# Low parts of the gate, branch, output and first MLP weights by an adding transfer from GpSimd

## Chip, cores, metric

One NeuronCore of a Trainium2 chip runs the whole program. The metric is device microseconds of one execution, the median of a few executions. Each execution computes one layer of a decoder for 512 tokens of width 1024 in float32.

## What is computed

Cut to the parts that the change touches; every product of activations and weights in it is a float32 matmul with inner dimension 512 or 1024.

```
h = rmsnorm(x, g_mix);  u = h @ w_in            # latents, pool, SSD, RG-LRU columns, and 4 x 1024 gate columns
y_a, y_b, y_c, y_d = attention, pooling, SSD, RG-LRU     # each 512 wide
gates = sigmoid(u[gate columns])
merged = sum over n of gates[n] * (y[n] @ w_branch[n])    # branch n: 512 x 1024
x = x + merged @ w_out
x = x + square(relu(rmsnorm(x, g_mlp) @ w_ff1)) @ w_ff2   # 1024 x 4096, 4096 x 1024
x = x + (p @ w_ple) * sigmoid(rmsnorm(x, g_ple) @ w_ple_gate)
out = rmsnorm(x, g_final)
```

## The kernel before

Every float32 matrix is split into a rounded part of type float32r, which TensorE takes at its fast rate, and the rest, also float32r: a = ah + al. A product is then three matmuls (helper `mm3`: high by high, high by low, low by high). In the trace they stand as lines L208, L209 and L210. Where the weight is the stationary operand, L208 and L209 read the weight's high tile `wh`, and only L210 reads its low tile `wl`.

The weights come in numbered units of 128 x 1024 (512 KB), in a fixed order (`UNITS`): latents, z and small projections, the gates of branch 0, the branch weights of 0 (`("br", 0, 0)` to `("br", 0, 3)`), then the LRU and pool projections mixed with the gates and branch weights of branch 2, then gates and branch weights of branches 3 and 1 in the pattern gate, branch, gate (one branch unit serves two output tiles), then 8 output units, then four chunks of the MLP. A chunk has 8 units of the first MLP matrix (`ff1`) and then a T phase: 14 units of the second matrix, which other code (`right_operand`, L192 and L193) splits from tiles `b` that SP loads. Units carry their number in the list below: 47 is the fourth gate of branch 2, 64 the second branch unit of branch 3, 70 its last, 87 the fourth output unit; 114, 136 and 158 are the first `ff1` units of chunks 1, 2 and 3, and 118 is the fifth of chunk 1.

`load_next` loads a unit: SP transfers it into `wr` (two buffers, L176), ScalarE rounds it into `wh` (three buffers, L177), VectorE subtracts, wl = wr - wh (three buffers, L178). `unit` calls it so that loading runs two units ahead of use. With three buffers of `wh` and `wl`, ScalarE can round a unit only once TensorE has left an older one. The framework decides the order on every engine beforehand from a modelled timeline, with the loads at high priority; each engine then runs its list strictly in order and waits on semaphores.

GpSimd (POOL) before has only elementwise work: the sum of the gated branches (L439), two products in the LRU and pooling (L764, L774, L805), and two differences of `b` tiles per quarter chunk for the T phase (L903, L904).

Of the kernel before, what the change touches and what calls it, by code (L numbers as in the profile page):

```python
# [10 lines left out]
F32 = mybir.dt.float32  # L11
F32R = mybir.dt.float32r
I32 = mybir.dt.int32
AF = mybir.ActivationFunctionType
ALU = mybir.AluOpType
# [37 lines left out]
UNITS = []  # L53
UIDX = {}
# [72 lines left out]
def trunk(tc, xT, pT, pos, par_d, cst_d, gfin, wblk_d, wpool_d, W, out, dbg=None):  # L127
    nc = tc.nc
    act, dve, pool, pe, sync = nc.scalar, nc.vector, nc.gpsimd, nc.tensor, nc.sync
    TAGS = {"G1": 16, "G2": 16, "G3": 16, "T1": 6, "T2": 8, "T3": 6, "Z": 4, "X": 8}  # L130
    BANKS = {"m": 3, "s": 2, "t": 2, "o": 1}
    with ExitStack() as ctx:
# [8 lines left out]
        def nm(s):  # L141
            cnt[0] += 1
            return f"{s}_{cnt[0]}"

        def A(tag, dt=F32, n="a"):
            return ap_.tile([P, S], dt, name=nm(n), tag=tag, bufs=TAGS[tag])
# [18 lines left out]
        def load_next():  # L165
            u = state[0]
            state[0] += 1
            n = UNITS[u][1]
            if UNITS[u][0][0] == "T":
                loaded[u] = right_operand(*UNITS[u][0][1:])  # L170
                return
            with tc.high_priority():
                raw = wp.tile([P, 1024], F32, name=nm("wr"), tag="wr", bufs=2)
                hi = wp.tile([P, 1024], F32R, name=nm("wh"), tag="wh", bufs=3)
                lo = wp.tile([P, 1024], F32R, name=nm("wl"), tag="wl", bufs=3)
                sync.dma_start(out=raw[:, :n], in_=W[u, :, :n])  # L176
                act.copy(out=hi[:, :n], in_=raw[:, :n])  # L177
                dve.tensor_tensor(out=lo[:, :n], in0=raw[:, :n], in1=hi[:, :n].bitcast(F32), op=ALU.subtract)  # L178
            loaded[u] = (hi, lo)


# [3 lines left out]
        def right_operand(ch, name, v):  # L185
            hi = wp.tile([P, 1024], F32R, name=nm("wh"), tag="wh", bufs=3)
            lo = wp.tile([P, 1024], F32R, name=nm("wl"), tag="wl", bufs=3)
            with tc.high_priority():
                for u in range(2):
                    kp, c = 2 * v + u, slice(u * S, (u + 1) * S)  # L190
                    src = ff2_raw[ch, {"t2": "b11", "t3": "b12", "t4": "b21"}.get(name, name), kp]
                    act.copy(out=hi[:, c], in_=src)  # L192
                    dve.tensor_tensor(out=lo[:, c], in0=src, in1=hi[:, c].bitcast(F32), op=ALU.subtract)  # L193
                    if name == "b11":
                        dve.tensor_tensor(out=src, in0=ff2_raw[ch, "b22", kp], in1=ff2_raw[ch, "t1", kp], op=ALU.subtract)
                    elif name == "b21":
                        dve.tensor_tensor(out=src, in0=src, in1=ff2_raw[ch, "b11", kp], op=ALU.subtract)
            return hi, lo

        def unit(*key):  # L200
            u = UIDX[key]
            while state[0] <= min(u + LOOK, NRING - 1):
                load_next()
            return loaded.pop(u)
# [16 lines left out]
        def pc(name, i=0, w=1):  # L221
            o, _ = PAR[name]
            return par[:, o + i:o + i + w]
# [93 lines left out]
        for k in range(KD):  # L317
            if k:
                sync.dma_start(out=xres[k], in_=xT[:, k, :])
            if k < 3:  # L320
                load_next()
            if k == 2:
                sync.dma_start(out=cst, in_=cst_d)
            xg.append(split_scaled(xres[k], pc("gmix", k), "G1", "xg"))
            q = A("T3", F32, "sq")
            act.activation(out=q, in_=xres[k], func=AF.Square)
            if acc is None:
                acc = q
            else:
                dve.tensor_tensor(out=acc, in0=acc, in1=q, op=ALU.add)  # L330
        for k in range(KD):
            if k == 5:
                with tc.high_priority():
                    vx = SM(NT, "vx")
                    dve.tensor_scalar(out=vx, in0=token_sums(acc), scalar1=1.0 / D, scalar2=EPS,
                                      op0=ALU.mult, op1=ALU.add)
                    rxb = bcast_tokens(rsqrt(vx, NT), "T1")
            w = loaded.pop(UIDX[("lat", k)])
            for i in range(5):
                c = slice(i * P, (i + 1) * P)  # L340
                mm3(lat_ps[i], w[0][:, c], w[1][:, c], xg[k][0], xg[k][1], k == 0, k == KD - 1)
            if k + 3 < KD:
                load_next()
# [7 lines left out]
        for k in range(KD):  # L351
            n = A("T3", F32, "hn")
# [118 lines left out]
        for t in range(NT):  # L471
# [3 lines left out]
                          in1=pc("dtb", 0, 8).unsqueeze(1).to_broadcast([P, NT, 8]), op=ALU.add)  # L475
# [75 lines left out]
        for hd in range(H):  # L551
# [11 lines left out]
            for kt in range(NT):  # L563
                pt = PS("t")
                n = S - kt * P
# [22 lines left out]
            else:  # L588
# [11 lines left out]
                                 in1=ah.unsqueeze(1).to_broadcast([P, NT, 8]), op0=ALU.mult, op1=ALU.mult)  # L600
# [18 lines left out]
        def bc8(v, n=8):  # L619
            return v.unsqueeze(2).to_broadcast([v.shape[0], n, 64])  # L620
# [4 lines left out]
        def csl(c):  # L625
            return slice(c * P, (c + 1) * P)
# [19 lines left out]
        for g in range(2):  # L646
            ps = PS("s")
            gs = slice(g * 64, g * 64 + 64)
            for c in range(NT):
                pe.matmul(ps[:, csl(c)], lhsT=xbc[4][gs, csl(c)], rhs=xbc[5][gs, csl(c)], start=True, stop=True)  # L650
            dve.tensor_tensor(out=heads(cbm[g], P), in0=heads(ps, P), in1=U.unsqueeze(1).to_broadcast([P, NT, P]),
                              op=ALU.mult)
        gate(0, 6, "G1")
        for c in range(NT):
            for g in range(2):
# [4 lines left out]
                for j in range(4):  # L660
# [4 lines left out]
                                   in1=cbm[g][:, csl(c)].unsqueeze(1).to_broadcast([P, 4, P]), op=ALU.mult)  # L665
# [4 lines left out]
        for c in range(NT - 1):  # L670
# [5 lines left out]
            for g in range(2):  # L676
# [4 lines left out]
                else:  # L681
                    dve.tensor_tensor(out=heads(Rn[gs, 0:256]), in0=heads(R[c][gs, 0:256]),
                                      in1=bc8(etot[gs, c * 8 + g * 4:c * 8 + g * 4 + 4], 4), op=ALU.mult)
# [3 lines left out]
        for c in range(NT):  # L687
# [7 lines left out]
            if c > 0:  # L695
                for g in range(2):
# [5 lines left out]
                                      in1=bc8(eacs[:, c * 8 + g * 4:c * 8 + g * 4 + 4], 4), op=ALU.mult)  # L702
# [93 lines left out]
        for i in range(4):  # L796
            w = unit("pool", i)
            ps = proj(w, hh, KD)
            u = A("T3", F32, "pu")
            act.copy(out=u, in_=ps)  # L800
            src = u
            n = 1
# [148 lines left out]
        for hf in range(2):  # L951
            ws = []
            for k in range(KD):
                raw = A("T1", F32, "pgw")
# [11 lines left out]
        for hf in range(2):  # L966

            for j in range(0, KD, 2):
                ps = PS("t")
                for u in range(2):  # L970
                    for t in range(2):
                        k = j + u
                        pe.transpose(out=ps[:, (2 * u + t) * P:(2 * u + t + 1) * P],
                                     in_=xt[2 * hf + t][k // 4][:, (k % 4) * P:(k % 4 + 1) * P], identity=ident)
# [28 lines left out]
        for hf in range(2):  # L1003
            ws = pgs[hf]
            for t in range(NT):
# [6 lines left out]
                for q in range(nf):  # L1012
# [3 lines left out]
                    for k in range(KD):  # L1016
# [9 lines left out]
                                                          in1=gf[:, hf, c], op=ALU.mult)  # L1026
# [146 lines left out]
```

## Time and profile before

| | |
|---|---|
| median of 3 runs | 981.22 us (980.24 to 982.66) |
| profiled execution | 982.21 us, its span 980.4 us: 1.8 us lie around the span |
| TensorE busy | 954.9 us, 97% of the span |
| VectorE, ScalarE, GpSimd busy | 661.4, 489.4 and 138.8 us |
| transfers | 96.95 MB, 29.5% of 16 DMA engines' time on SP's queue |

The share of the span says how much of the time an engine had work; the waits say what it waited for otherwise. Matmul ends are modelled, so TensorE's pace is better read from the starts of its rows.

### The profile page before, as it was taken

What the parts mean: (1) busy time and instruction counts of PE and PEld (TensorE: products, weight loads), DVE (VectorE), ACT (ScalarE), POOL (GpSimd) and SP (SyncE); (2) the same over time, 40 slices, a digit from 0 to 9 for tenths busy, and PEclk for the clock granted to TensorE, in tenths of its full rate; (3) what the DMA queues carried; (4) which work ended last, traced back from release to release, by engine and by line L of the source; (5) the groups of instructions that cost most, each with busy time, mean ns of one, the idle gap of its engine ahead of it and who ended that gap; (6) DMA issues with size and microseconds to landing.
All of it is one profiled execution on the core that took longest, in us unless ns stands there. A gap on an engine that the chain in (4) does not pass through costs nothing.

```text
span 980.4 us, 12002 instructions
## 1 busy us (share of the span) xinstructions
PE 954.9 (97%) x4389; PEld 782.4 (80%) x4389; DVE 661.4 (67%) x1156; ACT 489.4 (50%) x860; POOL 138.8 (14%) x107
## 2 busy tenths in 40 slices
PE   7999999999999999999999999999999999999996
PEld 5877788877777887788888888788887888887785
DVE  7768787557885753443433656996897789689636
ACT  6755777768276333222332435543543453456633
POOL 0000000005102423311122001350013005000021
PEclk9999999999999999999999999999999999999998
DMA  5423221214112332332324326134133304424002
GB/s 201 136 76 103 78 74 65 66 44 151 65 65 86 119 108 84 108 108 87 129 86 151 108 76 226 65 129 150 65 101 126 108 31 142 139 81 134 1 1 86
DMA packets 36473, 96.95 MB, mean 99 GB/s; under 512 B 4768, under 2 KB 4800, under 8 KB 36416
## 3 DMA queue, kind: packets, MB, share of 16 engines
q1 hardware_dynamic: 35472, 95.35, 29.5%
q10 hardware_dynamic: 944, 0.85, 0.3%
q8 instruction: 34, 0.56, 0.2%
q14 instruction: 23, 0.19, 0.1%
HBM read 94.01 MB, written 2.18 MB: 98 GB/s over the span
## 4 chain that ended last, share of the span: by engine, by line
PE 81%; DVE 13%; ACT 2%; issue 2%; DMA 2%; ACTq 0%; DVEq 0%
PE psm L208 21%; PE psm L210 21%; PE psm L209 21%; DVE wl L193 4%; PE pss L208 3%; PE pss L209 3%; PE pss L210 3%; DVE xtok L894 2%; DVE wl L178 1%; PE pst L567 1%; PE pst L209 1%; PE pst L208 1%; PE pso L210 1%; PE pso L208 1%; PE pso L692 1%
## 5 line engine op out<-in xcount | busy, mean ns | idle before, releaser
L177 ACT CAST wh<-wr 128x1024 fp32r<-128x1024 f32 (+3 forms) x126 | 128.7, 1023 | 227.3 <-PE psm L209 148.5
L178 DVE TENSOR_TENSOR wl<-wr,wh 128x1024 fp32r<-128x1024 f32 (+3 forms) x126 | 157.6, 1254 | 112.2 <-ACT wh L177 105.3
L208 PE MATMUL psm<-hh,wh 128*128 128x512 f32 (+1 forms) x408 | 161.5, 396 | 0.3 <-DVE rot L459 0.3
L209 PE MATMUL psm<-hl,wh 128*128 128x512 f32 (+1 forms) x408 | 161.0, 395 | 0.0
L210 PE MATMUL psm<-hh,wl 128*128 128x512 f32 (+1 forms) x408 | 159.3, 390 | 0.0
L210 PE MATMUL psm<-x2h,wl 128*128 128x512 f32 x256 | 100.0, 391 | 0.8 <-DVE wl L178 0.8
L208 PE MATMUL psm<-x2h,wh 128*128 128x512 f32 x256 | 99.9, 390 | 0.0
L209 PE MATMUL psm<-x2l,wh 128*128 128x512 f32 x256 | 99.9, 390 | 0.0
L209 PEld LDWEIGHTS psm<-hl,wh 128*128 128x128 f32 (+1 forms) x408 | 76.2, 187 | 18.4 <-issue 2.5
L208 PEld LDWEIGHTS psm<-hh,wh 128*128 128x128 f32 (+1 forms) x408 | 76.2, 187 | 18.3 <-issue 1.5
L210 PEld LDWEIGHTS psm<-hh,wl 128*128 128x128 f32 (+1 forms) x408 | 76.2, 187 | 17.3 <-issue 1.3
L193 DVE TENSOR_TENSOR wl<-b,wh 128x512 fp32r<-128x512 f32 x96 | 84.1, 922 | 1.8 <-ACT wh L192 1.6
L192 ACT CAST wh<-b 128x512 fp32r<-128x512 f32 x96 | 54.4, 618 | 56.1 <-PE pss L210 30.5
L439 POOL TENSOR_TENSOR gth<-gth,gth 128x512 f32<-128x512 f32 x24 | 36.8, 1534 | 188.4 <-DVE gth L435 188.4
L903 POOL TENSOR_TENSOR t<-b,b 128x512 f32<-128x512 f32 x16 | 25.1, 1575 | 239.9 <-DVE xtok L894 163.7
L210 PEld LDWEIGHTS psm<-x2h,wl 128*128 128x128 f32 x256 | 48.1, 188 | 11.5 <-DVE wl L178 1.7
L209 PEld LDWEIGHTS psm<-x2l,wh 128*128 128x128 f32 x256 | 48.1, 188 | 9.9
L208 PEld LDWEIGHTS psm<-x2h,wh 128*128 128x128 f32 x256 | 48.1, 188 | 9.8
L921 DVE SCALAR_TENSOR_TENSOR ffr<-psm,bc 128x512 f32<-128x512 f32 x32 | 21.8, 688 | 33.9 <-PE psm L210 30.6
L638 POOL TENSOR_TENSOR xsd<-xt,par 128x512 f32<-128x512 f32 x4 | 5.5, 1392 | 224.5 <-ACT xt L634 224.5
L435 DVE SCALAR_TENSOR_TENSOR gth<-gth,psm 128x512 f32<-128x512 f32 x32 | 21.9, 685 | 14.9 <-PE psm L210 14.8
L1025 POOL TENSOR_TENSOR xtok<-xtok,gf 128x512 f32<-128x512 f32 x7 | 9.0, 1289 | 134.4 <-ACT pth L1024 134.4
(398 smaller groups left out, 2084.9 us busy)
## 6 DMA issues: line engine op xcount, KB each, us to landing
wr<-W SPq DMA_DIRECT2D x114, 512.0 KB, 3.3
b<-W SPq DMA_DIRECT2D x64, 256.0 KB, 3.4
pgw<-W SPq DMA_DIRECT2D x16, 256.0 KB, 2.9
x<-xT SPq DMA_DIRECT2D x15, 256.0 KB, 5.2
wr<-W SPq DMA_DIRECT2D x8, 320.0 KB, 3.6
E<-acd SPq DMA_DIRECT2D x8, 256.0 KB, 4.4
out<-xtok SPq DMA_DIRECT2D x8, 256.0 KB, 2.1
wr<-W SPq DMA_DIRECT2D x3, 384.0 KB, 2.9
```

The lines of the kernel that those rows point to most:

```text
L177: act.copy(out=hi[:, :n], in_=raw[:, :n])
L178: dve.tensor_tensor(out=lo[:, :n], in0=raw[:, :n], in1=hi[:, :n].bitcast(F32), op=ALU.subtract)
L192: act.copy(out=hi[:, c], in_=src)
L193: dve.tensor_tensor(out=lo[:, c], in0=src, in1=hi[:, c].bitcast(F32), op=ALU.subtract)
L208: pe.matmul(ps, lhsT=s_h, rhs=m_h, start=first, stop=False, **kw)
L209: pe.matmul(ps, lhsT=s_h, rhs=m_l, start=False, stop=False, **kw)
L210: pe.matmul(ps, lhsT=s_l, rhs=m_h, start=False, stop=last, **kw)
L435: dve.scalar_tensor_tensor(out=th, in0=th, scalar=1.0, in1=pb, op0=ALU.add, op1=ALU.mult)
L439: pool.tensor_tensor(out=merged[j], in0=merged[j], in1=th, op=ALU.add)
L894: dve.tensor_tensor(out=xt[t0 + t][hf], in0=xt[t0 + t][hf], in1=banks[t], op=ALU.add)
L903: pool.tensor_tensor(out=t1, in0=b12, in1=b11, op=ALU.subtract)
L921: dve.scalar_tensor_tensor(out=r, in0=ps, scalar=0.0, in1=rb, op0=ALU.max, op1=ALU.mult)
```

## The change

For 79 of the units (24 gates, 15 branch units, 8 output units, 32 `ff1` units) VectorE's subtraction goes. ScalarE, after rounding, writes the negated high part into the low tile, and GpSimd issues a transfer that reads the unit a second time from DRAM and adds it onto that tile: wl = -wh + w. The first transfer into `wr` and the rounding stay, and so do the other units.

```diff
                 sync.dma_start(out=raw[:, :n], in_=W[u, :, :n])
                 act.copy(out=hi[:, :n], in_=raw[:, :n])
-                dve.tensor_tensor(out=lo[:, :n], in0=raw[:, :n], in1=hi[:, :n].bitcast(F32), op=ALU.subtract)
+                if UNITS[u][0][0] in ("gate", "br", "out", "ff1") and u > UIDX["br", 0, 0]:
+                    act.activation(out=lo[:, :n], in_=hi[:, :n].bitcast(F32), func=AF.Copy, scale=-1.0)
+                    pool.dma_start(out=lo[:, :n], in_=W[u, :, :n], accum_op=ALU.add)
+                else:
+                    dve.tensor_tensor(out=lo[:, :n], in0=raw[:, :n], in1=hi[:, :n].bitcast(F32), op=ALU.subtract)
```

Lines behind it move by 4, so L208 to L210 are L212 to L214 in the changed kernel, and L903 and L904 are L907 and L908.

The framework orders the engines anew. On GpSimd, at the end of chunk 0's T phase, where the differences for chunk 1 stand (t1 and b12 are tiles of the second MLP matrix), this stood before:

```order
L903 TENSOR_TENSOR t1_1289_5992<-b12_1287_5988,b11_1285_5984 128x512
L904 TENSOR_TENSOR b12_1263_5888<-b22_1264_5890,b12_1263_5888 128x512
L904 TENSOR_TENSOR b12_1287_5988<-b22_1288_5990,b12_1287_5988 128x512
L903 TENSOR_TENSOR t1_1345_6370<-b12_1343_6366,b11_1341_6362 128x512
L904 TENSOR_TENSOR b12_1343_6366<-b22_1344_6368,b12_1343_6366 128x512
```

and this stands now (wl_1211 is the low tile of unit 114, wl_1214 that of 115):

```order
L907 TENSOR_TENSOR t1_1289_6055<-b12_1287_6051,b11_1285_6047 128x512
L908 TENSOR_TENSOR b12_1263_5949<-b22_1264_5951,b12_1263_5949 128x512
L908 TENSOR_TENSOR b12_1287_6051<-b22_1288_6053,b12_1287_6051 128x512
L180 DMA wl_1211_5703<-W 128x1024
L180 DMA wl_1214_5722<-W 128x1024
```

The adding transfers of the chunk's units stand behind all eight differences; chunks 2 and 3 begin in the same way.

On ScalarE, in the gates and branch units of branch 3, before (wh_877 is the high tile of unit 64, wh_883 that of 65, gth_880 a gate):

```order
L177 CAST wh_877_3807<-wr_876_3806 128x1024
L428 ACTIVATE gth_880_3837<-psm_879_3812 128x512
L177 CAST wh_883_3855<-wr_882_3854 128x1024
L177 CAST wh_888_3888<-wr_887_3887 128x1024
L428 ACTIVATE gth_886_3885<-psm_885_3860 128x512
```

and now:

```order
L177 CAST wh_877_3826<-wr_876_3825 128x1024
L432 ACTIVATE gth_880_3857<-psm_879_3832 128x512
L177 CAST wh_883_3875<-wr_882_3874 128x1024
L179 ACTIVATE wl_878_3827<-wh_877_3826 128x1024
L179 ACTIVATE wl_884_3876<-wh_883_3875 128x1024
```

The negation for unit 64 stands behind the rounding of unit 65. For unit 87 it is alike: rounding of 88, then two activations of 128 x 512 for the residual (L296, L281), then the negation for 87. In most other units the negation follows its own rounding directly or with one short activation between.

On TensorE, at the start of chunk 1, before (psm_1223 is the product of unit 114 with wh_1210 and wl_1211):

```order
L208 MATMUL psm_1223_5703<-x2h_1043_4872,wh_1210_5647 128x512
L209 MATMUL psm_1223_5703<-x2l_1044_4873,wh_1210_5647 128x512
L210 MATMUL psm_1223_5703<-x2h_1043_4872,wl_1211_5648 128x512
L208 MATMUL psm_1223_5703<-x2h_1045_4876,wh_1210_5647 128x512
L209 MATMUL psm_1223_5703<-x2l_1046_4877,wh_1210_5647 128x512
```

and now:

```order
L212 MATMUL psm_1223_5761<-x2h_1043_4921,wh_1210_5702 128x512
L213 MATMUL psm_1223_5761<-x2l_1044_4922,wh_1210_5702 128x512
L212 MATMUL psm_1228_5796<-x2h_1043_4921,wh_1213_5721 128x512
L213 MATMUL psm_1228_5796<-x2l_1044_4922,wh_1213_5721 128x512
L214 MATMUL psm_1223_5761<-x2h_1043_4921,wl_1211_5703 128x512
L212 MATMUL psm_1223_5761<-x2h_1045_4925,wh_1210_5702 128x512
```

Two matmuls of the next unit, which need no low part, stand ahead of the first use of `wl`. The same holds for units 64 and 87. At unit 47 the twelve matmuls of a branch product stand ahead of it.

## Rows read from the trace of the kernel before

**Rows 1.** Head of the page: span, and busy time of each engine.
```profile
span 980.4 us, 12002 instructions
PE 954.9 (97%) x4389; PEld 782.4 (80%) x4389; DVE 661.4 (67%) x1156; ACT 489.4 (50%) x860; POOL 138.8 (14%) x107
```

**Rows 2.** What TensorE waited for: us in total, times, longest.
```profile
PE psm L208 <- ACT wh L177: 7.0, 1, 7.0
...
PE psm L210 <- DVE wl L178: 0.8, 2, 0.4
...
PE pst L209 <- DVE wl L193: 0.7, 1, 0.7
```

**Rows 3.** Busy time in stretches: PE, PEld, DVE, ACT, POOL, clock, DMA share, GB/s.
```profile
500.00:550.00 50.00, 50.00 (x222) 41.42 (x221) 22.05 (x26) 18.15 (x24) 9.04 (x5) 1.00 0.36 120
...
600.00:650.00 50.00, 48.88 (x222) 39.80 (x222) 44.71 (x70) 25.65 (x47) 12.94 (x10) 1.00 0.36 117
...
800.00:850.00 50.00, 49.41 (x217) 40.27 (x216) 41.83 (x53) 20.27 (x31) 12.66 (x8) 1.00 0.41 129
```

**Rows 4.** VectorE's subtraction, full units: count, busy us, mean ns, idle before.
```profile
L178 DVE TENSOR_TENSOR wl<-wr,wh 128x1024 fp32r<-128x1024 f32 x114 | 147.4, 1296 | 108.9 <-ACT wh L177 102.0 <-PE pst L790 5.5
```

**Rows 5.** DMA: SP's queue (packets, MB, share of 16 engines); one issue's KB and landing.
```profile
q1 hardware_dynamic: 35472, 95.35, 29.5%
...
wr<-W SPq DMA_DIRECT2D x114, 512.0 KB, 3.3
```

**Rows 6.** Timeline of GpSimd and ScalarE at three chunk starts, and a lone GpSimd sum.
```profile
507.63 1.29 POOL L439 TENSOR_TENSOR gth<-gth,gth 128x512 f32<-128x512 f32 x1 [5.83 <-DVE gth L435]
...
658.56 3.45 POOL L904 TENSOR_TENSOR b<-b,b 128x512 f32<-128x512 f32 x2
...
740.17 3.44 POOL L904 TENSOR_TENSOR b<-b,b 128x512 f32<-128x512 f32 x2
740.25 1.06 ACT L177 CAST wh<-wr 128x1024 fp32r<-128x1024 f32 x1 [1.58 <-PE pst L210]
...
822.96 3.44 POOL L904 TENSOR_TENSOR b<-b,b 128x512 f32<-128x512 f32 x2
```

**Rows 7.** Timeline of TensorE: first use of the low tiles of units 114, 136, 158.
```profile
663.87 0.39 PE L210 MATMUL psm<-x2h,wl 128*128 128x512 f32 x1
...
746.55 0.50 PE L210 MATMUL psm<-x2h,wl 128*128 128x512 f32 x1 [0.43 <-DVE wl L178]
...
829.33 0.50 PE L210 MATMUL psm<-x2h,wl 128*128 128x512 f32 x1 [0.40 <-DVE wl L178]
```

**Rows 8.** Units 64 and 87: roundings of 65 and 88, and first use of 64's, 87's low tiles.
```profile
416.74 1.05 ACT L177 CAST wh<-wr 128x1024 fp32r<-128x1024 f32 x1 [1.18 <-PE psm L209]
...
422.66 0.39 PE L210 MATMUL psm<-ydh,wl 128*128 128x512 f32 x1
...
541.90 1.05 ACT L177 CAST wh<-wr 128x1024 fp32r<-128x1024 f32 x1
543.20 0.72 ACT L296 ACTIVATE x2h<-x,par 128x512 fp32r<-128x512 f32 x1 [0.24 <-DVE x L842]
...
547.78 0.39 PE L210 MATMUL psm<-mgh,wl 128*128 128x512 f32 x1
```

**Rows 9.** Unit 47: GpSimd's four LRU products, and first use of the low tile.
```profile
315.67 6.41 POOL L764 TENSOR_TENSOR xc<-xc,m 128x512 f32<-128x512 f32 x4 [1.43 <-ACT m L762]
...
323.83 0.39 PE L210 MATMUL psm<-hh,wl 128*128 128x512 f32 x1
```

**Rows 10.** Even running: rounding and first use of the low tile, units 70 and 118.
```profile
446.66 1.05 ACT L177 CAST wh<-wr 128x1024 fp32r<-128x1024 f32 x1 [6.62 <-PE psm L209]
...
455.30 0.39 PE L210 MATMUL psm<-ydh,wl 128*128 128x512 f32 x1
...
674.31 1.05 ACT L177 CAST wh<-wr 128x1024 fp32r<-128x1024 f32 x1 [3.77 <-PE psm L209]
...
685.63 0.39 PE L210 MATMUL psm<-x2h,wl 128*128 128x512 f32 x1
```

## Prediction

> **What bounds the kernel now.** I read the head of the page first. TensorE is busy 954.9 of 980.4 us [rows 1], so time can only be won where it stands still, and is lost wherever something new makes it stand. Then the waits: behind VectorE's subtraction, the instruction that goes, TensorE waited 0.8 us, in two places, the starts of chunks 2 and 3; behind VectorE's other subtraction (T phase, not changed) 0.7 us; the one long wait, 7.0 us, is for the first rounding of the program and is not touched [rows 2]. The stretches say the same: around 500 us, in the middle of gates and branch units, TensorE is full at 222 matmuls in 50 us, so a unit of 24 matmuls lasts 5.4 us; the T phases of 600 to 650 and 800 to 850 us leave 1.1 and 0.6 us idle, with VectorE at 45 and 42 of 50 us [rows 3]. So VectorE's load is high only where the change takes nothing away.
>
> **What goes.** 79 subtractions at a mean of 1.3 us [rows 4] are 102 us of VectorE, and all but 0.8 us of them lie under matmuls. Their going is worth 0 to 0.8 us; I take 0, because in those two places the new transfer stands where the subtraction stood.
>
> **What comes.** 79 negations on ScalarE. The nearest row, the rounding of the same shape, takes 1.05 us [rows 10]: 83 us on an engine that is busy half of the span [rows 1]. They cost nothing by themselves; the cover is the two units of lookahead, and their place in the chain to `wl` is the subtraction's, 0.2 us shorter. And 79 adding transfers of 512 KB that GpSimd issues, behind which GpSimd's own sums queue; that is covered too, since a sum has to be done only before the next branch's sum onto the same tile, eight outputs later.
>
> **X, the price of one adding transfer**, from the end of the negation to a usable `wl`, is in no row. From below: a plain transfer of the same size from SP lands 3.3 us after its issue [rows 5]. From above: two such in a row plus one GpSimd instruction, for which the nearest row is a sum of 1.3 us [rows 6], 7.9 us. Between: to add, something must also read the 512 KB that lie in SBUF. SP's queue used 29.5% of 16 engines' 980.4 us for 95.35 MB [rows 5], so 0.524 MB cost 1.6 us of all engines; 3.3 + 1.6, and 0.6 for GpSimd's handling (between SP's, which is in the 3.3, and 1.3), gives **X = 5.5 us**. That a second pass costs time is certain, that it is not overlapped at all is not, and GpSimd may be slower; so I keep 3.3 and 7.9 as the ends.
>
> The 1.6 us for the second read stand on rows 5. The Trainium skill, in "Collectives: The Full Stack", section "The bandwidth ceiling: the fold count and why AG ≠ RS ≠ AR", says that an add in the DMA engines costs no cycles itself but needs two source reads on one ring, and so runs at half the rate of a copy. No run so far shows that here; by it alone (X = 4.9) the sum below would be 8.5 us.
>
> **What waits for it.** I call lead the time from when GpSimd can issue a unit's transfer to when TensorE first uses `wl`. A unit costs X minus lead where that is positive. A stall shifts all that follows, releases of buffers too, so stalls add.
>
> In even running the lead is long. Unit 118: rounding ends at 675.4, one short activation, negation done by 677.1, first use 685.6 [rows 10]: 8.6 us. A branch unit in the gate, branch, gate pattern, unit 70: rounding and negation end at 448.8, first use 455.3 [rows 10]: 6.5 us. So most of the 79 cost nothing at 5.5 us. The order of the engines makes six exceptions:
>
> - Starts of chunks 1, 2 and 3. GpSimd has the T-phase differences ahead of the transfer until 658.56 + 3.45 = 662.0, 743.6 and 826.4 us [rows 6]; rounding and negation of unit 136 are through at 740.25 + 2 × 1.06 = 742.4 [rows 6], so GpSimd decides. TensorE's first use was at 663.87, 746.55 and 829.33 [rows 7], plus 0.45 for the two matmuls now ahead of it (50 us / 222 each). Leads 2.3, 3.4, 3.4; stalls at 5.5: 3.2 + 2.1 + 2.1 = 7.4 us.
> - Unit 64: its negation follows the rounding of 65, which waits for TensorE and ends at 417.8 [rows 8]; done 418.85; first use 422.66 + 0.45. Lead 4.3, stall 1.2 us.
> - Unit 87: behind the rounding of 88 (ends 542.95) and two activations of 0.7 and 0.6 us [rows 8], negation done at 545.3; first use 547.78 + 0.45. Lead 3.0, stall 2.5 us.
> - Unit 47: GpSimd's four LRU products end at 322.1 [rows 9] and stand ahead of it; first use 323.83 plus twelve matmuls, 2.7 us. Lead 4.5, stall 1.0 us.
>
> **Sum**: 7.4 + 1.2 + 2.5 + 1.0 = 12.1 us on the profiled execution's 982.2: 994.3. That execution lies 1.0 us above the median of the runs, so I predict **993 us**. At X = 3.3 the same sum is 1.3 us, at 7.9 it is 26.5, plus 1.4 us for each of seven further branch units: 36 us, 1018.
>
> **Engine time.** A changed unit needs 1.6 us of the 16 engines for its first load and, with two reads, 3.2 for the add: 4.8 of 5.4 us. It fits, but barely.
>
> **Rivals.**
> *The add is hidden.* X below 3.7 costs under 3 us by the six leads, 981 to 984 us, no change to be told (a measurement of this kernel tells 0.3%, 2.9 us). For it: 3.3 us for the plain transfer, and the raw buffer is now free 1.3 us earlier, after the rounding, so that raw loads and adds meet less. Against it: the second read. The Trainium skill, "DMA: Bandwidth & Descriptors", section "Anatomy of one DMA — SWDGE (gpsimd) path", fits a transfer from GpSimd as 2.0 us plus its bytes over 436 GB/s, an estimate of 3.2 us here, and does not speak of adding ones; by it the time would be that of this rival, 983. I give 0.13.
>
> *Every branch unit stalls.* X from 6.5 to 8.5: the leads of 6.5 are used up: at 6.5 the six leads cost 18 us, at 8.5 they cost 30 and the seven branch units 14, so 999 to 1024. For it: the upper bound, and that raw loads and adds share 16 engines. 0.18.
>
> *The DMA engines become the bound.* If an add takes over 3.8 us of all engines (2.4 plain ones), load and add exceed 5.4 us, and the 64 units that stand in unbroken runs (24 of branches 3 and 1, 8 output, 32 `ff1`) run at the engines' pace: at 5 us, 64 × 1.2 = 77 us, 1059. For it: 4.8 of 5.4 is close, and no row shows the rate of an add. 0.14.
>
> *Faster.* VectorE, freed of 102 us, enters the T phases without backlog and TensorE's idle time there goes: 1.1 us in the first, 0.6 in each of the other three [rows 3], 2.9 us: 978.3 by the median. It needs X below 2.3, the shortest lead; the plain transfer's 3.3 speaks against it, and so does that the subtraction, where it did sit at the end of a T phase, cost TensorE only 0.8 us [rows 2]. 0.05.
>
> **How the numbers follow.** Forecast (X from 3.7 to 6.5, 984 to 999 us) 0.50, the rivals 0.13, 0.18, 0.14, 0.05. Faster by over 0.3%: 0.05; within 0.3%: 0.13; slower: 0.82. The range leaves out the faster case below and most of the engine-bound case above, 983 to 1055; the forecast's own is 984 to 999.
>
> **What would show it.** Right: waits of TensorE's L214 for a DMA into `wl` of 2 to 4 us at the three chunk starts, 1 to 3 us at units 64 and 87, hardly any between; issue to landing on GpSimd's queue near 5 us; DMA share in the gates rising from 0.36 to about 0.65 to 0.9; VectorE's busy time down by some 100 us. The hidden case shows landings near 3.3 us and no such waits. Waits at each branch unit mean X over 6.5; DMA share near 1 and waits at all units mean the engines. I am wrong if landings are far from 5 us, or if the stalls sit elsewhere: at the end of attention, where three negations (units 33 to 35) join a busy ScalarE, which I cost at nothing, or in GpSimd's sums.

## Result and the profile after

The changed kernel takes 1027.9 us (median of 4 runs, 1026.5 to 1030.0) against 981.3 us, a ratio of 1.0474 [1.0461, 1.0487]: 46.6 us slower. The profiled execution took 1026.8 us, its span 1024.8 us, 44.4 us more than before [rows 1].

Head of the page after:

```profile
span 1024.8 us, 12203 instructions
...
PE 970.1 (95%) x4389; PEld 790.8 (77%) x4389; DVE 566.0 (55%) x1077; ACT 565.6 (55%) x939; POOL 201.2 (20%) x186
```

VectorE lost 95 us of work, and TensorE's idle time rose from 25.5 to 54.7 us; its busy time rose too, by 15 us, for the same 4389 matmuls. What TensorE waited for, after (in total, times, longest):

```profile
PE psm L214 <- DMA wl<-W: 29.6, 8, 5.8
PE psm L212 <- ACT wh L177: 6.8, 2, 6.4
```

The second row stood there before [rows 2]; the first is new. The eight waits in the timeline of TensorE (start, us, instruction, and in brackets the wait before it), which are units 47, 64, 87, 95, 99, 114, 136 and 158 by the order of the transfers:

```profile
331.34 0.50 PE L214 MATMUL psm<-hh,wl 128*128 128x512 f32 x1 [2.47 <-DMA wl<-W]
...
431.12 0.50 PE L214 MATMUL psm<-ydh,wl 128*128 128x512 f32 x1 [2.92 <-DMA wl<-W]
...
559.36 0.80 PE L214 MATMUL psm<-mgh,wl 128*128 128x512 f32 x1 [2.63 <-DMA wl<-W]
...
611.46 0.79 PE L214 MATMUL psm<-x2h,wl 128*128 128x512 f32 x1 [4.03 <-DMA wl<-W]
...
641.33 0.80 PE L214 MATMUL psm<-x2h,wl 128*128 128x512 f32 x1 [2.88 <-DMA wl<-W]
...
693.33 0.80 PE L214 MATMUL psm<-x2h,wl 128*128 128x512 f32 x1 [5.75 <-DMA wl<-W]
...
783.08 0.79 PE L214 MATMUL psm<-x2h,wl 128*128 128x512 f32 x1 [4.70 <-DMA wl<-W]
...
872.00 0.79 PE L214 MATMUL psm<-x2h,wl 128*128 128x512 f32 x1 [4.26 <-DMA wl<-W]
```

Where the matmul behind the wait lasts 0.8 us and not 0.5, TensorE runs at half its clock. The stretches behind the last six waits (us, busy time and matmuls of TensorE, PEld, VectorE, ScalarE and GpSimd, then granted clock, DMA share, GB/s):

```profile
559.40:562.50 3.10, 3.10 (x7) 2.44 (x8) 0.37 (x1) 0.00 (x0) 0.00 (x0) 0.50 1.03 262
611.50:617.10 5.60, 5.60 (x13) 4.41 (x14) 0.69 (x2) 0.41 (x1) 0.00 (x0) 0.50 1.06 265
641.30:644.40 3.10, 3.07 (x7) 2.48 (x8) 3.10 (x4) 0.10 (x1) 2.61 (x2) 0.50 0.04 16
693.30:699.00 5.70, 5.67 (x13) 4.46 (x14) 0.00 (x0) 0.00 (x0) 0.00 (x0) 0.50 0.80 181
783.10:787.70 4.60, 4.60 (x11) 3.63 (x12) 0.00 (x0) 0.00 (x0) 0.00 (x0) 0.50 1.07 255
872.00:876.50 4.50, 4.50 (x11) 3.53 (x12) 0.00 (x0) 0.00 (x0) 0.00 (x0) 0.50 1.06 259
```

Granted 0.50 is 1.2 GHz of 2.4. In 26.6 us stand 62 matmuls; at the pace of before, 222 in 50 us [rows 3], they need 14.0. So the clock costs 12.6 us, and 29.6 + 12.6 = 42.2 of 44.4 us. The starts of TensorE's matmuls, compared one by one in order with those before, place most of the rest: TensorE lags by nothing at 197 us, by 1.4 us at 310, by 44.4 at 900 and by 44.2 at 1014, and between the eight places the lag does not grow. So the eight places cost 43 us, and 1.5 us were lost between 200 and 285 us, where units 33 to 40 are loaded. No new wait stands there; why TensorE is slower is not shown.

The DMA queues and issues after:

```profile
q1 hardware_dynamic: 35472, 95.35, 27.8%
q0 software_dynamic: 11376, 41.42, 23.5%
...
wr<-W SPq DMA_DIRECT2D x114, 512.0 KB, 3.4
wl<-W POOLq DMA_DIRECT2D x79, 512.0 KB, 5.7
```

The median landing of the adding transfers is 5.7 us, where X was put at 5.5. But a median of 79 says little about the eight that were waited for. Issue to landing of all 79 (L180), and of unit 114's alone:

```profile
DMA to landing us min/median/max: 5.2/5.7/11.8
...
DMA to landing us min/median/max: 8.7/8.7/8.7
```

The stretch from 500 us on of [rows 3], after:

```profile
500.00:550.00 50.00, 50.00 (x222) 41.16 (x221) 8.08 (x12) 23.32 (x28) 13.96 (x14) 1.00 0.88 206
```

In the gates TensorE is as full as before, 222 matmuls in 50 us, although the DMA share rose from 0.36 to 0.88: there a nearly full set of DMA engines costs TensorE nothing by itself.

Place by place. The lead is the start of the wait (row's start minus the bracket) minus the start of GpSimd's issue in its timeline:

```profile
323.48 0.87 POOL L180 DMA_DIRECT2D wl<-W  x1
...
424.95 1.81 POOL L180 DMA_DIRECT2D wl<-W  x2
...
553.67 0.86 POOL L180 DMA_DIRECT2D wl<-W  x1 [10.03 <-ACT wl L179]
...
601.89 1.81 POOL L180 DMA_DIRECT2D wl<-W  x2 [10.33 <-ACT wl L179]
...
632.66 0.88 POOL L180 DMA_DIRECT2D wl<-W  x1
...
684.56 0.88 POOL L180 DMA_DIRECT2D wl<-W  x1
...
775.35 0.87 POOL L180 DMA_DIRECT2D wl<-W  x1
...
864.73 0.88 POOL L180 DMA_DIRECT2D wl<-W  x1
```

| unit | lead forecast | lead measured | landing (forecast 5.5) | wait forecast | wait measured |
|---|---|---|---|---|---|
| 47 | 4.5 | 5.4 | 7.8 | 1.0 | 2.5 |
| 64 | 4.3 | 3.3 | 6.1 | 1.2 | 2.9 |
| 87 | 3.0 | 3.1 | 5.6 | 2.5 | 2.6 |
| 95 | none given | 5.5 | 9.5 | 0 | 4.0 |
| 99 | none given | 5.8 | 8.6 | 0 | 2.9 |
| 114 | 2.3 | 3.0 | 8.7 | 3.2 | 5.8 |
| 136 | 3.4 | 3.0 | 7.7 | 2.1 | 4.7 |
| 158 | 3.4 | 3.0 | 7.2 | 2.1 | 4.3 |

At the six forecast places the leads are right within 1.1 us, and their errors cancel. The landings are not: they sum to 43.2 us in place of 6 × 5.5 = 33. What stands in the way is SP's queue:

```profile
323.56 0.33 SPq L953 DMA_DIRECT2D gf<-gfin  x1
...
601.05 2.63 SPq L903 DMA_DIRECT2D b<-W  x5
...
627.51 6.94 SPq L903 DMA_DIRECT2D b<-W  x7
...
682.30 5.80 SPq L176 DMA_DIRECT2D wr<-W  x3
...
685.02 0.33 SPq L176 DMA_DIRECT2D wr<-W  x1
```

Around unit 95's issue at 601.89 SP sends five `b` tiles of 256 KB, around 99's seven, and around 114's the raw loads of three later units; the last row is the second of these three by itself, 0.46 us behind GpSimd's issue. And 0.08 us behind 47's issue SP sends the 512 KB of `gf`, the gain of the last norm. Summed from the packet records of the trace, in KB per us, for the stretch around unit 114:

```
us       684  685  686  687  688  689  690  691  692
SP       304   20  128  228  116    8    8   88  132
GpSimd     0    0    0    0   84  188  204  148  140
```

The transfer issued at 684.56 moves nothing until the raw load issued at 685.02 is nearly through. An undisturbed adding transfer moves its first bytes 1.6 us after its issue, this one after 3.6. At 47, 95, 99, 136 and 158 it is 4.1, 3.8, 2.4, 3.0 and 3.7 us, and at each of these six SP issues a load within 0.6 us of GpSimd's issue, before or behind. Where SP's next load comes 1.0 us or more behind (units 44, 60, 77 and 84, and 118 and 142 with over 3 us), the first bytes come after 1.6 to 1.7 us and the landing after 5.2 to 6.7. Units 35 and 85, which nobody waited for, had late first bytes too, 4.1 and 3.8, behind five or six SP loads issued before. That is read from this one trace; the time between the two issues was not varied by itself.

The Trainium skill, "DMA: Bandwidth & Descriptors", section "Queues, rings and completion order", says that an engine takes turns between the queues it has work for, but drains a whole packet of one before it switches. The 2 us in which unit 114's transfer gets no turn would fit that if an engine's whole share of a load counted as one packet, which no run here shows.

### The profile page after: what moved, and what is told of

The parts are those of the page before. It is cut to its first block, busy times and chain, and to the rows that moved or that the text cites. A ratio compares the mean times of both kernels' runs of the same rounds, so it can differ in the third digit from the quotient of the medians.

```text
span 1024.8 us, 12203 instructions
## 1 busy us (share of the span) xinstructions
PE 970.1 (95%) x4389; PEld 790.8 (77%) x4389; DVE 566.0 (55%) x1077; ACT 565.6 (55%) x939; POOL 201.2 (20%) x186
## 3 DMA queue, kind: packets, MB, share of 16 engines
q0 software_dynamic: 11376, 41.42, 23.5%
## 4 chain that ended last, share of the span: by engine, by line
PE 78%; DMA 8%; DVE 6%; issue 4%; ACT 2%; POOL 1%; ACTq 0%; SPq 0%; POOLq 0%; DVEq 0%
PE psm L214 20%; PE psm L212 19%; PE psm L213 19%; DMA wl<-W 6%; PE pss L212 3%; PE pss L213 3%; PE pss L214 3%; PE pst L212 1%; DMA wr<-W 1%; PE pst L213 1%; PE pst L214 1%; PE pst L571 1%; PE pso L214 1%; PE pso L696 1%; PE pso L212 1%
## 5 line engine op out<-in xcount | busy, mean ns | idle before, releaser
L214 PE MATMUL psm<-hh,wl 128*128 128x512 f32 (+1 forms) x408 | 160.0, 392 | 2.5 <-DMA wl<-W 2.5
L212 PE MATMUL psm<-hh,wh 128*128 128x512 f32 (+1 forms) x408 | 161.6, 396 | 0.3 <-DVE rot L463 0.3
L180 POOL DMA_DIRECT2D wl<-W x79 | 68.6, 868 | 474.5 <-ACT wl L179 466.7
L214 PE MATMUL psm<-x2h,wl 128*128 128x512 f32 x256 | 105.2, 413 | 21.6 <-DMA wl<-W 21.6
L212 PE MATMUL psm<-x2h,wh 128*128 128x512 f32 x256 | 103.9, 406 | 0.0
L213 PE MATMUL psm<-x2l,wh 128*128 128x512 f32 x256 | 103.6, 405 | 0.0
L214 PEld LDWEIGHTS psm<-hh,wl 128*128 128x128 f32 (+1 forms) x408 | 76.3, 187 | 20.0 <-DMA wl<-W 2.9
L212 PEld LDWEIGHTS psm<-hh,wh 128*128 128x128 f32 (+1 forms) x408 | 76.2, 187 | 18.5 <-issue 2.0
L179 ACT ACTIVATE wl<-wh 128x1024 fp32r<-128x1024 f32 x79 | 83.0, 1053 | 1.4 <-ACT y L709 0.6
L214 PEld LDWEIGHTS psm<-x2h,wl 128*128 128x128 f32 x256 | 50.8, 199 | 34.4 <-DMA wl<-W 23.8
L182 DVE TENSOR_TENSOR wl<-wr,wh 128x1024 fp32r<-128x1024 f32 (+3 forms) x47 | 54.0, 1150 | 35.8 <-ACT wh L177 35.4
L213 PEld LDWEIGHTS psm<-x2l,wh 128*128 128x128 f32 x256 | 50.6, 198 | 11.3
L212 PEld LDWEIGHTS psm<-x2h,wh 128*128 128x128 f32 x256 | 51.1, 199 | 10.6
L907 POOL TENSOR_TENSOR t<-b,b 128x512 f32<-128x512 f32 x16 | 25.6, 1606 | 107.3 <-DVE xtok L898 72.9
L443 POOL TENSOR_TENSOR gth<-gth,gth 128x512 f32<-128x512 f32 x24 | 32.0, 1332 | 72.4 <-DVE gth L439 71.9
```

Source lines behind the costliest of these rows:

```text
L179: act.activation(out=lo[:, :n], in_=hi[:, :n].bitcast(F32), func=AF.Copy, scale=-1.0)
L180: pool.dma_start(out=lo[:, :n], in_=W[u, :, :n], accum_op=ALU.add)
L212: pe.matmul(ps, lhsT=s_h, rhs=m_h, start=first, stop=False, **kw)
L213: pe.matmul(ps, lhsT=s_h, rhs=m_l, start=False, stop=False, **kw)
L214: pe.matmul(ps, lhsT=s_l, rhs=m_h, start=False, stop=last, **kw)
L443: pool.tensor_tensor(out=merged[j], in0=merged[j], in1=th, op=ALU.add)
```

## Experiments

Where a kernel changes part of the computation, its paragraph says which. Ratios are to the kernel before; "half" counts the stretches at the half clock apart from the last one, in which the program ends before the change too. In three kernels (eight units out, transfer without add, spare tile) one of them stands behind a wait of 2.0 us for VectorE at the start of the first T phase.

| kernel | median us | ratio [95%] | us of waits for transfers into `wl` | half |
|---|---|---|---|---|
| changed | 1027.9 | 1.0474 [1.0461, 1.0487] | 29.6 in 8 | 6 |
| no adds in the first MLP | 998.9 | 1.017 [1.0155, 1.0186] | 9.9 in 3 | 3 |
| eight waited-for units out | 1011.1 | 1.030 [1.0269, 1.033] | 16.2 in 7 | 4 |
| GpSimd transfer without add | 1003.7 | 1.0229 [1.0207, 1.025] | 13.0 in 6 | 5 |
| subtraction 4 times, no adds | 988.1 | 1.0069 [1.0046, 1.0091] | none | 0 |
| adds into a spare tile | 987.4 | 1.0062 [1.0049, 1.0076] | none | 1 |
| adds without raw loads | 1009.3 | 1.0284 [1.0268, 1.0301] | 17.1 in 8 | 3 |
| subtraction 8 times, no adds | 990.7 | 1.0096 [1.008, 1.0112] | none | 1 |
| 37 units in even running | 993.3 | 1.0115 [1.0098, 1.0131] | 9.0 in 6 | 1 |
| subtraction 16 times, no adds | 1021.6 | 1.0394 [1.0365, 1.0423] | none | 7 |
| 19 units | 981.9 | 1.0001 [0.9992, 1.001] | none | 0 |

**No adds in the first MLP.**

```diff
-                if UNITS[u][0][0] in ("gate", "br", "out", "ff1") and u > UIDX["br", 0, 0]:
+                if UNITS[u][0][0] in ("gate", "br", "out") and u > UIDX["br", 0, 0]:
```

> Only the 47 gate, branch and output units keep the adding transfer; the 32 units of the first MLP matrix are subtracted on VectorE as before. Theory (eight waits, and a halved clock behind six of them): the waits at units 47, 64 and 87 stay, 2.5 + 2.9 + 2.6 = 8.0 us, and one stretch of 3.4 us at the half clock behind the third, worth 1.7 us: about 991 us, and no stretch at the half clock after 565 us but the last one. Rival (every adding transfer costs its share of 46.6 / 79 = 0.59 us, by traffic or by queues): 47 x 0.59 = 28 us, 1009 us.

998.9 us, between the 991 of the theory and the 1009 of the rival. The same three units wait, 47 for 2.7, 64 for 4.7 and 87 for 2.6 us, and no other transfer is waited for, so the loss sits in places and not in every transfer: these waits and three stretches at the half clock make some 15 of the 17 us. But the clock fell behind each of the three, not only behind the last, and unit 64's transfer landed after 7.9 us in place of 6.1: both sizes vary from kernel to kernel.

**The eight waited-for units out.**

```diff
-                if UNITS[u][0][0] in ("gate", "br", "out", "ff1") and u > UIDX["br", 0, 0]:
+                if UNITS[u][0][0] in ("gate", "br", "out", "ff1") and u > UIDX["br", 0, 0] and u not in (47, 64, 87, 95, 99, 114, 136, 158):
```

> 71 of the 79 units keep the adding transfer; the eight at whose low tile TensorE waited (47, 64, 87, 95, 99, 114, 136, 158) are subtracted on VectorE. Theory (the eight waits and the clock behind them are the whole loss): 981 to 985 us, a little above before if the next unit, whose transfer took 9 to 12 us behind the first one, now stands alone in front. Rival (71 x 0.59 us): 1023 us. Rival of the clock (the transfers bring it down, not the standing still): the half clock stays and costs its 17 us, 998 us.

1011.1 us: my theory, in the form that these eight units were the whole loss, fell. The waits moved to their neighbours. Two of the seven in TensorE's timeline, units 49 and 116:

```profile
345.45 0.80 PE L214 MATMUL psm<-hh,wl 128*128 128x512 f32 x1 [5.58 <-DMA wl<-W]
...
693.38 0.79 PE L214 MATMUL psm<-x2h,wl 128*128 128x512 f32 x1 [3.03 <-DMA wl<-W]
```

Unit 116's transfer was issued 4.4 us ahead of its first use and landed after 7.4; 138 and 160 had leads of 6.5 and 7.9 and landed after 9.1 and 9.0. In the changed kernel the wait of the chunk's first unit had pushed back their first use too. The waits of 16.2 us and the four stretches at the half clock make some 23 of the 29.5 us; the rest is not placed.

**GpSimd's transfer without the add** (the low tile then holds the whole weight).

```diff
-                    pool.dma_start(out=lo[:, :n], in_=W[u, :, :n], accum_op=ALU.add)
+                    pool.dma_start(out=lo[:, :n], in_=W[u, :, :n])
```

> All 79 transfers stay on GpSimd in the same order behind the same negation, but do not add: the low tile then holds the whole weight, so the products are not the reference's. Theory (the second read is what makes the price, as the prediction had it: 1.6 us of 5.5): issue to landing in the undisturbed units falls from 5.2-5.5 to about 3.7 us, the eight waits lose 1.6 us or more each, 29.6 to about 13 us, and the clock falls behind the longest of them only: 995 to 1005 us. Rival (GpSimd's own handling makes the price): landing stays over 5 us and the time at 1028 us.

1003.7 us, as expected, though the clock fell behind four of the six waits and not behind the longest alone. Its DMA queues and issues:

```profile
q0 software_dynamic: 11376, 41.42, 13.0%
...
wl<-W POOLq DMA_DIRECT2D x79, 512.0 KB, 4.5
```

One plain transfer takes 13.0% × 1005.1 / 79 = 1.65 us of all engines, an adding one 23.5% × 1024.8 / 79 = 3.05. Undisturbed it lands after 3.4 to 3.8 us, an adding one after 5.2 to 5.5. So the add is paid in full, in engine time and in landing, by about what the prediction put down for a second read. The read itself is not seen: the queue's bytes are the same 41.42 MB in both kernels.

The Trainium skill, in "Collectives: The Full Stack", section "The bandwidth ceiling: the fold count and why AG ≠ RS ≠ AR", has the add of a collective run at half the rate of a copy; the trace agrees nearly, with 3.05 against 1.65. The Trainium skill's fit in "DMA: Bandwidth & Descriptors", section "Anatomy of one DMA — SWDGE (gpsimd) path", an estimate of 3.2 us here, comes near the 3.4 to 3.8 of a plain transfer that nothing disturbs, and is far from the 5.2 to 5.5 of an adding one.

**The subtraction several times, without adds**: does standing still alone bring the clock down?

```diff
-                dve.tensor_tensor(out=lo[:, :n], in0=raw[:, :n], in1=hi[:, :n].bitcast(F32), op=ALU.subtract)
+                for _ in range(4 if u in (87, 114, 136, 158) else 1):
+                    dve.tensor_tensor(out=lo[:, :n], in0=raw[:, :n], in1=hi[:, :n].bitcast(F32), op=ALU.subtract)
```

> The kernel before, no adding transfer at all, but VectorE does the subtraction of units 87, 114, 136 and 158 four times over, so that the low tile comes 3.9 us later. Theory of the clock (TensorE's standing still for some 3 to 6 us is enough): waits of about 4 us at 114, 136 and 158 and of 0 to 3 us at 87, 12 to 15 us in all, and behind each of the long ones a stretch at the half clock of 3.4 to 6.8 us, worth 1.7 to 3.4 us each: 998 to 1008 us. Rival (the adding transfers bring the clock down): the same waits, no stretch at the half clock but the last: 993 to 996 us.

988.1 us, and undecided: VectorE began early, and the waits for the low tile were 1.0 to 1.3 us only. The same with 8:

> As the kernel with the subtraction four times over, but eight times, at units 87, 114, 136 and 158: the low tiles of the last three come 5.2 us later still, no adding transfer anywhere. Theory of the clock (standing still is enough): waits of about 6 us at each of the three and 0 to 5 us at 87, 18 to 23 us in all, and behind each a stretch at the half clock, worth 1.7 to 3.4 us each: 1006 to 1018 us. Rival (the adding transfers bring the clock down): the waits alone, 999 to 1004 us, and no stretch at the half clock but the last.

990.7 us; waits of 1.1, 2.4 and 1.0 us, and one fall, behind the 2.4. In windows: the wait itself, the matmuls behind it, and on:

```profile
749.90:752.10 2.20, 0.00 (x0) 0.00 (x0) 2.20 (x3) 0.00 (x0) 0.00 (x0) 1.00 0.00 0
...
753.90:757.10 3.20, 3.20 (x8) 2.47 (x8) 2.96 (x3) 0.52 (x1) 0.00 (x0) 0.50 0.30 120
757.30:765.00 7.70, 7.70 (x36) 6.32 (x35) 6.55 (x6) 2.01 (x3) 0.00 (x0) 1.00 0.31 108
```

With 16:

> As the two kernels with repeated subtractions and no adding transfer, now sixteen times at units 87, 114, 136 and 158, since VectorE began the eight early and the waits were only 1.0 to 2.4 us, with one stretch at the half clock, behind the wait of 2.4. Theory of the clock (standing still is enough): waits of 5 us or more at three places at least, and behind each of them a stretch at the half clock in which matmuls start 0.43 us apart in place of 0.23. Rival (the one stretch was chance, and the adding transfers bring the clock down): waits as long, no such stretch but at the end.

1021.6 us. The waits came elsewhere and shorter than expected (VectorE's backlog holds up ScalarE and the MLP's own steps), but seven stretches at the half clock followed, behind waits of 1.8 to 4.9 us. The longest wait, the matmuls behind it and what came next:

```profile
917.00:921.60 4.60, 0.00 (x0) 0.00 (x0) 3.50 (x8) 2.90 (x5) 0.00 (x0) 0.79 0.45 151
921.70:926.40 4.70, 4.70 (x11) 3.59 (x12) 3.86 (x8) 2.36 (x5) 0.00 (x0) 0.50 0.34 112
926.60:940.00 13.40, 13.40 (x61) 11.12 (x60) 13.40 (x23) 8.44 (x16) 0.00 (x0) 1.00 0.45 144
```

11 matmuls in 4.7 us, then 61 in 13.4: no adding transfer is needed for it. The rival, that the adding transfers bring the clock down, is out.

**Adds into a spare tile.** VectorE subtracts as before; negation and transfer go where nobody reads.

```diff
-                    act.activation(out=lo[:, :n], in_=hi[:, :n].bitcast(F32), func=AF.Copy, scale=-1.0)
-                    pool.dma_start(out=lo[:, :n], in_=W[u, :, :n], accum_op=ALU.add)
-                else:
+                    side = spare[0][:, u % 2, :]
+                    act.activation(out=side[:, :n], in_=hi[:, :n].bitcast(F32), func=AF.Copy, scale=-1.0)
+                    pool.dma_start(out=side[:, :n], in_=W[u, :, :n], accum_op=ALU.add)
+                if True:
```

> From unit 64 on (60 units) negation and adding transfer are all there, on the same engines and queues, but go into a spare tile that nobody reads; VectorE makes the low tile by the subtraction as before. Theory (the loss is TensorE's waiting for the low tile, and the clock behind it): no wait for a transfer, no stretch at the half clock but the last, 981 to 986 us. Rival (the second read, 31 MB more, takes the DMA engines from the other loads, or ScalarE and GpSimd hold up what stands behind): 60 x 0.59 = 35 us, 1017 us; half of it would still be 999.

987.4 us, just above what was expected and far from the rival. TensorE waits 2.0 us for VectorE at the start of the first T phase (longer than before), and a little for ScalarE; one stretch at the half clock, which was not expected, stands behind the 2.0 us. And this although the transfers land late:

```profile
spare<-W POOLq DMA_DIRECT2D x60, 512.0 KB, 7.9
```

So for 60 of the 79 units 31 MB more on the DMA engines and the negations on ScalarE cost up to 6 us together; the rest of what the adding transfers cost is the waiting.

**Adds without raw loads.** From unit 64 on SP's load goes and the high part is rounded from an old tile. The low tile, the weight minus that part, makes up for it, but the split is a coarser one, so those products are not quite the reference's.

```diff
+                alone = UNITS[u][0][0] in ("gate", "br", "out", "ff1") and u > 63
+                raw = keep[0] if alone else wp.tile([P, 1024], F32, name=nm("wr"), tag="wr", bufs=2)
...
-                sync.dma_start(out=raw[:, :n], in_=W[u, :, :n])
+                if not alone:
+                    sync.dma_start(out=raw[:, :n], in_=W[u, :, :n])
```

> From unit 64 on the first load of a changed unit is left out (its high part is rounded from an old tile, so these products are not the reference's); the 60 adding transfers stay. Theory (the landing of 6 to 9 us at the places that waited is an adding transfer of 5.2 to 5.5 us queued behind loads of later units in the same engines): landing 5.2 to 5.6 us wherever two adds don't follow each other closely; units 95 and 99 (leads 5.5 and 5.8) wait no more; 64, 87, 114, 136 and 158 (leads of 3.0 to 3.3) wait 2.0 to 2.5 each; with unit 47's 2.5 that is about 14 us, and some 6 us for the clock: 1000 us. Rival (the landing is long there for GpSimd's sake, or by the adds alone): landings and waits as they were, 1025 us.

1009.3 us against 1000 expected and 1025 by the rival. The landings did what the theory says: unit 114's fell from 8.7 us to

```profile
DMA to landing us min/median/max: 5.6/5.6/5.6
```

and those of 64, 87, 95, 136 and 158 from 5.6-9.5 to 5.3-5.5. Unit 95 waits no more, and 136 and 158 wait as X minus lead says, 5.4 - 3.0:

```profile
769.49 0.50 PE L218 MATMUL psm<-x2h,wl 128*128 128x512 f32 x1 [2.51 <-DMA wl<-W]
...
854.29 0.50 PE L218 MATMUL psm<-x2h,wl 128*128 128x512 f32 x1 [2.41 <-DMA wl<-W]
```

Unit 114 still waits 3.2 us, since its lead here is 2.5. Two of the eight land late as before, both beside loads of SP that stay: 99 after 7.7 us (wait 1.6), with the packets of SP's `b` loads just ahead of its own, and 47 after 8.0, with `gf` issued 0.08 us behind it. Neither load was taken away by itself. Waits of 17.1 us and three stretches at the half clock are some 22 us; a few us more are not placed.

**37 units in even running, and 19.**

```diff
-                if UNITS[u][0][0] in ("gate", "br", "out", "ff1") and u > UIDX["br", 0, 0]:
+                if u in (*range(66, 84), *range(88, 95), *range(118, 122), *range(140, 144), *range(162, 166)):
```

> Only units in even running keep the adding transfer: 66 to 83, 88 to 94 and the last four of the first MLP's eight in chunks 1 to 3, 37 in all; the others are subtracted on VectorE. Theory (where the lead exceeds 6 to 8 us the transfer costs nothing): 980 to 985 us. Rival (waits move on to whichever unit is then first behind a pause, as in the kernel with eight units taken out): 2 to 5 us and a stretch at the half clock at units 66, 118, 140 and 162: 995 to 1010 us.

Of 88 to 94, the units to 91 are of the output, 92 to 94 of the first MLP. 993.3 us: the rival was nearer, though at other units than it named. Branch unit 67 waited 2.6 us (landing 9.0, lead 6.5), and five gates 1.0 to 1.7. In the new order GpSimd issues two transfers 2.4 us apart, and the second, the gate's, lands after 7.4 to 8.0 us with a lead of 6.4. No unit from 88 on waited. With those 19 alone (the first range left out):

> 19 units keep the adding transfer: 88 to 94 of the output and the last four of the first MLP's eight in chunks 1 to 3, none of which was waited for in the kernel with 37. Theory (a transfer that lands before its first use costs nothing): no wait for a transfer, 980 to 984 us. Rival (each transfer costs something by traffic, by the negation on ScalarE or by GpSimd): 19 x 0.59 = 11 us, 993 us. Nothing speaks for faster than 979: VectorE's subtraction was waited for 0.8 us in the kernel before.

981.9 us, 1.0001 [0.9992, 1.001]. No wait for a transfer is left, and these 19 transfers are free within the interval. Nor is anything won.

## Why the prediction was off

The direction, the mechanism and six of the eight places were right; the size was not: +12 us forecast, +46.6 measured, inside the range of 983 to 1055, but far beyond the forecast's own, 984 to 999.

- **Term "X, the price of one adding transfer", 5.5 us: the step that failed, worth 17.1 us** (10.2 at the six places, 6.9 at two others)**.** As the price of one undisturbed transfer it held (5.2 to 5.5; median of all 5.7), and so did its parts: 1.4 us more engine time for the add, where 1.6 was forecast for a second read. The error was to put one X into all leads. The leads are short where other work stands ahead of the transfer, at the starts of the chunks above all, and at four of the six places SP issues a load of its own at the same moment. The landings were 5.6 to 8.7 us at the six places, worth 10.2 us more. I had written that raw loads and adds "meet less"; the kernel without raw loads shows them meeting at 64, 114, 136 and 158; at 47 it is another load of SP that stands beside the transfer.
- **"Most of the 79 cost nothing"**: of the 73 outside the six places, 71 did; 95 and 99 cost 6.9 us. Unit 95's landing fell from 9.5 to 5.3 us in the kernel without raw loads, where by the packet records SP moves nothing from 599 to 609 us. For 99 the `b` tiles beside it fit, in both kernels, but they were not taken away alone.
- **No term for the clock**, the second step that failed: 12.6 us. The sum counted a wait as lost once, and nothing in the prediction says why no more. Six of the eight are paid again in matmuls at 1.2 GHz.
- The account: 12.1 forecast + 10.2 (landings) + 0.4 (leads, and 0.04 us a wait from landing to matmul) + 6.9 (two new places) = 29.6; + 12.6 (clock) = 42.2 of 44.4 us. Of the other 2.2, 1.5 were lost before the first of the eight places.
- **Engine time**, 1.6 + 3.2 of 5.4 us: measured 3.05 for the add, and TensorE full at a DMA share of 0.88. The rival of the DMA engines did not come.
- **Every branch unit stalls**: not in the changed kernel; in the one with 37 units one branch unit and five gates waited, the gates by two transfers close together, which the rival did not name.
- **The add is hidden**: not even a transfer without an add is; at 3.4 us undisturbed it still cost 13.0 us of waits and 22 us in all, for the same reason as X.
- **Faster**: VectorE's 95 us bought nothing, as [rows 2] said; the kernel with 19 units, with 21 us less on VectorE, shows it at 0.0%.
- **End of attention (units 33 to 35) and GpSimd's sums, put at nothing**: TensorE has no new wait there. But the 1.5 us between 200 and 285 us were lost around the end of attention, for a reason that is not shown.

## What to carry to other kernels

A price taken from a transfer's median landing is too low where it matters: leads are shortest at changes of phase and behind other work, and there other queues' loads are in flight. Read at each short lead what the other queues issue around it, above all at the same moment, and count a wait of TensorE as possibly paid twice, once standing and once at the half clock behind it. And taking out the units that wait moves the wait to the next one; work moves off an engine for nothing if TensorE did not wait for that engine.

## What was not expected of the hardware

After a wait of over 3 us the granted clock fell in every case here (ten waits, 3.0 to 5.8 us, the program's start aside). After waits of 1.8 to 2.9 us it fell in some and not in others: not behind unit 47's 2.5 and unit 64's 2.9 in the changed kernel, and in the one with sixteen subtractions behind one wait of 1.8 us but not behind another. Stretches at the half clock lasted 3.4 or 6.8 us, and the long ones began 1.1 to 2.3 us before the wait ended. And in the changed kernel two adding transfers issued 1 to 3 us apart land 2.3 to 4.3 us apart, so that unit 96, issued 1.0 us behind 95, landed 11.8 us after its issue.
